# Row maxima of two softmaxes, taken straight from PSUM and turned into a row by one product with ones

## The chip, the cores and the metric

The kernel runs on one core of a Trainium2 chip. The metric is the device time of one execution in microseconds (us), lower is better. TensorE multiplies matrices, VectorE (DVE) and ScalarE (ACT) work on tiles in SBUF and PSUM, GpSimd (POOL) on tiles in SBUF, and DMA queues move data between SBUF and device memory.

## The reference

One layer over 2048 latent tokens and 256 context tokens, width 1024. All tokens are normalised, modulated and projected. Two attentions run on the result: latent attention (MLA, 8 heads, 96 score dimensions, keys are 2048 latent and 256 context tokens) and 2-D neighbourhood attention on a 32 x 64 grid (8 heads, a window of 8 x 16 keys with a learned bias, and all context keys). Both are gated, projected, merged and projected again, then a residual and a norm follow.

```python
def one(qblk):                       # latent attention, one block of queries
    sc = jnp.einsum('bqhd,bkhd->bhqk', qblk, k) * scale
    p = jax.nn.softmax(sc, axis=-1)
    return jnp.einsum('bhqk,bkhd->bqhd', p, v)

# neighbourhood attention, one grid row
s_win = jnp.einsum('bwhd,brwchd->bhwrc', qr, k_win) * scale + bias
s_ctx = jnp.einsum('bwhd,blhd->bhwl', qr, kc) * scale
p = jax.nn.softmax(jnp.concatenate([s_win, s_ctx], axis=-1), axis=-1)
```

## The kernel before, in words

Until about 1062 us the kernel normalises, modulates and projects. From there to about 2255 us stands the attention stretch: both attentions in one stream. After it come the gated output products.

A number is kept as a high and a low part of type fp32r, and a score is the sum of three products (high by high, high by low, low by high).

**Latent attention** (loop at L1242). 32 blocks u, each one head and 512 queries (g). A block has nine key steps kp of 2 x 128 keys. In a step each half makes a transposed score tile S (keys on partitions, 512 queries wide) in PSUM by three products, ScalarE takes the exponential into a tile P (L1274), GpSimd adds P to the running denominator za (L1280, L1282), and every second step TensorE multiplies the collected P by the values (pv, L1225, into oacc). The softmax needs the maximum of each query. It enters the score as a 97th contraction row: the keys have a row of ones, and row 96 of the query tile qh holds minus the maximum. A block's scores can only start when this row is there.

The maxima of block u+1 are made during block u (max_tasks, L809, a list of 13 tasks). For each 128 queries (qt), the scores of high by high are made once more with queries on partitions (pm tiles, 512 keys wide, the last 256). `pair` (L820) makes two of them: ScalarE copies the first to SBUF (L823), VectorE takes a running maximum over the second and the copy (a scan, L825). `rest` (L828) reduces the last 256 keys (L830) and joins both (L831). `fin` (L834) first runs the deferred work (zdefer: the denominators' sums zp of an earlier block), then turns the four columns of maxima into a row by four fp32 products with the identity, L840, each shown as two instructions in the trace, and ScalarE copies the row into qh (L841).

**Neighbourhood attention** (natten, L1026). Per head, 16 query tiles have window products nm and context products nc, whose maxima VectorE takes (n_max, L878). `fin` (L906) joins them once (L908, L909), then turns the 16 columns into rows, four columns at a time (four products nf, L912), and VectorE copies each into QLt (L914). The maxima of head h+1 are made while head h is scored; the four `fin` items come at the start of a head. The work is a generator that yields weights; `feed` (L1167) takes from it twice per key step so that it is spread evenly over the stretch.

**Order.** In the stretch TensorE's matmuls (mm, L804) are pinned in program order. The other engines' instructions are ordered by the scheduler of the framework from priorities and dependences, and each engine then runs its own in order. `more` (L1260) issues the maxima's tasks through the steps of a block; `fin` falls into the last step, behind its first score. PSUM tiles of scores, maxima and neighbourhood scores take turns in five buffers (psm, L140). The maxima of block 0 are issued with a high priority (L1159) and run among the projections, around 863 to 880 us. SBUF space of the attention pools is partly that of the projections' operands.

Of the kernel before, what the change touches and what calls it, by code (L numbers as in the profile page):

```python
# [11 lines left out]
F32 = mybir.dt.float32  # L12
F32R = mybir.dt.float32r
AF = mybir.ActivationFunctionType
ALU = mybir.AluOpType
AX = mybir.AxisListType
# [3 lines left out]
P = 128  # L20
# [6 lines left out]
H = 8  # L27
# [5 lines left out]
DK = NOPE + ROPE  # L33
NB = 4
W = S // NB
NK = S + C
# [28 lines left out]
def tile_hybrid_layer(ctx: ExitStack, tc: tile.TileContext, I: dict, out: bass.AP, dbg=None):  # L65
    nc = tc.nc
# [8 lines left out]
    ident = const.tile([P, P], F32, name="ident")  # L75
# [64 lines left out]
    def psm(name):  # L140
        if env["rot"] is not None:
            env["rot"] = (env["rot"] + 1) % 5
            if env["rot"] >= 3:
                return env["psS"].tile([P, W], F32, tag="S", name=name)
        return psM.tile([P, W], F32, tag="M", name=name)
# [652 lines left out]
        nc.gpsimd.memset(bc(Kh[i][DK:DK + 1, :]), 1.0)  # L798

    zdefer = []  # L800

    pe = {"pin": False}

    def mm(*args, **kw):  # L804
        ins = nc.tensor.matmul(*args, **kw)  # L805
        if pe["pin"]:
            tc.keep_in_program_order(ins)

    def max_tasks(u, qh):  # L809
        i = (u // NB) % 2  # L810
        m1 = mq.tile([P, 4], F32, tag="m1", name=f"m1{u}")
        last = [None] * 4

        def product(qt, ci):
            a, b = ci * W, min(NK, (ci + 1) * W)
            pm = psm(f"pm{u}_{qt}_{ci}")
            mm(pm[:, :b - a], qh[0:DK, qt * P:(qt + 1) * P], Kh[i][0:DK, a:b], start=True, stop=True)
            return pm

        def pair(qt, ci):  # L820
            p0 = product(qt, ci)
            sb = mq.tile([P, W], F32, tag="msb", name=f"msb{u}_{qt}_{ci}")
            nc.scalar.activation(sb, p0, AF.Copy)  # L823
            p1 = product(qt, ci + 1)
            nc.vector.tensor_tensor_scan(sb, p1, sb, -3.0e38 if ci == 0 else last[qt], op0=ALU.max, op1=ALU.max)  # L825
            last[qt] = sb[:, W - 1:W]

        def rest(qt):  # L828
            p0 = product(qt, 4)
            nc.vector.tensor_reduce(m1[:, qt:qt + 1], p0[:, :NK - 4 * W], axis=AX.X, op=ALU.max, negate=True)  # L830
            nc.vector.scalar_tensor_tensor(out=m1[:, qt:qt + 1], in0=last[qt], scalar=-1.0, in1=m1[:, qt:qt + 1],  # L831
                                           op0=ALU.mult, op1=ALU.min)

        def fin():  # L834
            for f in zdefer:
                f()
            zdefer.clear()
            pm = psm(f"pmf{u}")
            for t in range(4):
                mm(pm[DK:DK + 1, t * P:(t + 1) * P], m1[:, t:t + 1], ident, start=True, stop=True)  # L840
            nc.scalar.activation(qh[DK:DK + 1, :], pm[DK:DK + 1, :], AF.Copy)  # L841

        o = []
        for qt in range(4):
            o += [lambda q=qt: pair(q, 0), lambda q=qt: pair(q, 2), lambda q=qt: rest(q)]
        return o + [fin]


    def grid(ap):
# [28 lines left out]
    def n_max(h, bn):  # L878
        mx = nv.tile([P, 2, 16], F32, tag="nmx", name=f"nmx{h}")
        m1 = nv.tile([P, 16], F32, tag="nm1", name=f"nm1{h}")  # L880
        kg = grid(NKm[:, 0:S])
        neg = -3.0e38

        def win(qb):
            rb, cb = divmod(qb, 4)
            (r0, r1), (c0, c1) = NROW[rb], CREG[cb]
            nr, ncl = r1 - r0, c1 - c0
            pm = psm(f"nm{h}_{qb}")
            pv_ = pm[:, :nr * ncl].rearrange("p (r c) -> p r c", c=ncl)
            mm(pv_, NQs[:, qb * P:(qb + 1) * P], kg[:, r0:r1, c0:c1], start=True, stop=True)  # L890
            rr, cc_ = r0 - rb * 8 + 4, c0 - cb * 16 + 8
            jk = npl.tile([P, W], F32, tag="njk", name=f"njk{h}_{qb}", bufs=1)
            nc.vector.tensor_tensor_reduce(
                out=jk[:, :nr * ncl].rearrange("p (r c) -> p r c", c=ncl), in0=pv_,
                in1=bn[:, rr:rr + nr, cc_:cc_ + ncl], scale=1.0, scalar=neg,
                op0=ALU.add, op1=ALU.max, accum_out=mx[:, 0, qb:qb + 1])

        def cmax(b2):
            pm = psm(f"nc{h}_{b2}")
            for x in range(2):  # L900
                qb = 2 * b2 + x
                mm(pm[:, x * C:(x + 1) * C], NQs[:, qb * P:(qb + 1) * P], NKm[:, S:NK],
                                 start=True, stop=True)
            nc.vector.reduce_max(mx[:, 1, 2 * b2:2 * b2 + 2], pm.rearrange("p (x c) -> p x c", x=2), axis=AX.X)

        def fin(rb):  # L906
            if rb == 0:
                nc.vector.tensor_tensor(m1, mx[:, 0, :], mx[:, 1, :], op=ALU.max)  # L908
                nc.vector.tensor_scalar_mul(m1, m1, -1.0)  # L909
            pm = psm(f"nf{h}_{rb}")  # L910
            for cb in range(4):
                mm(pm[64:65, cb * P:(cb + 1) * P], m1[:, rb * 4 + cb:rb * 4 + cb + 1], ident,  # L912
                                 start=True, stop=True)
            nc.vector.tensor_copy(rowcol(QLt[64:65, rb * W:(rb + 1) * W]), blk(pm[64:65, :]))  # L914

        o = []
        for b2 in range(8):
            o += [lambda q=2 * b2: win(q), lambda q=2 * b2 + 1: win(q), lambda b=b2: cmax(b)]
        return o + [lambda r=r: fin(r) for r in range(4)]

    def n_score(d, t):
        h = d["h"]
# [96 lines left out]
            npairs.append([("w", a, cb), ("w", b, cb)])  # L1019

    WT, WM, WI, WP = 1.0, 0.6, 6.0, 16
    n_weight = 24 * WM + H * (24 * WT + 24 * WM + 4 * WM + WI)

    held = []

# [131 lines left out]
    load_rope(1)  # L1157
    env["q"] = nc.sync
    with tc.high_priority(offset=HOIST):  # L1159
        for f in max_tasks(0, qhs[0]):  # L1160
            f()

    env["psS"], env["rot"] = psS, -1
# [78 lines left out]
    for u in range(nu):  # L1242
# [1 line left out]
        i = h % 2  # L1244
        qh, ql = qhs[u], qls[u]
        vt = Vt
        tasks = []
        if u + 2 < nu:
            qhs.append(load_qh(u + 2))
        if u + 1 < nu:  # L1250
            tasks = max_tasks(u + 1, qhs[u + 1])
        if g == NB - 1 and h + 1 < H:
            Vt = load_v(h + 1)
        acc = psO.tile([P, W], F32, tag="O", name=f"oacc{u}")
# [3 lines left out]
        for kp in range(NKP):  # L1258
            pt = mp.tile([P, 2, W], F32, tag="P", name=f"P{u}_{kp}", bufs=PB)
            def more(frac):  # L1260
                nonlocal done
                want = min(len(tasks), int(len(tasks) * (kp + frac) / (NKP - 0.7) + 1))
                while done < want:
                    tasks[done]()
                    done += 1

            for x in range(2):
                ks = slice((2 * kp + x) * P, (2 * kp + x + 1) * P)
                sp = psm(f"S{u}_{kp}_{x}")
                n = 0  # L1270
                for a, b, e in ((Kh[i], qh, DK + 1), (Kh[i], ql, DK), (Kl[i], qh, DK)):
                    mm(sp, a[0:e, ks], b[0:e, :], start=(n == 0), stop=(n == 2))
                    n += 1
                nc.scalar.activation(pt[:, x, :], sp, AF.Exp)  # L1274
                more(0.33 * x)
                if x == 0:
                    feed(total_weight * (step + 0.5 - LEAD) / (nsteps - TAIL - LEAD))
            ve = nc.vector if kp in ZDVE.get(nu - u, ()) else nc.gpsimd
# [259 lines left out]
```

## Time and profile before

| | |
|---|---|
| runs shown, us | 2628.12, 2628.84, 2633.1 (median 2628.84) |
| profiled execution, us | 2630.43, span of the profile 2628.6 |
| mean granted clock of TensorE | 0.994 |
| TensorE busy, share of the span | 2554.9 us, 97% |
| VectorE, ScalarE, GpSimd busy | 1246.7, 1038.4, 1029.1 us |
| instructions | 36044 |

The profiled execution is 1.6 us above the median of the runs. Matmuls overlap each other in the pipeline, so a matmul of 0.40 us duration can be followed by the next after less; the distance of the starts tells what one costs in a stream. A wait is put down to what ended last before the waiting instruction started.

### The profile page before, as it was taken

The numbers are of one execution on the slowest core, as the hardware profiler recorded it, in microseconds if no ns is written. First come the engines' busy times: TensorE is split into PE (matmuls) and PEld (weight loads), VectorE is DVE, ScalarE is ACT, GpSimd is POOL, SyncE is SP. The second block draws the span as 40 slices with busy tenths as digits, with TensorE's granted clock in tenths as the row PEclk, the third lists the DMA queues.
The fourth block names the chain that finished last, engine by engine and source line by source line (L and its number), as shares of the span: only waits on it lengthen the run. The fifth ranks groups of instructions, "written<-read, shape, count | busy, mean of one in ns | idle before, by whom it ended". The sixth has DMA issues, their size and how long they took to land.

```text
span 2628.6 us, 36044 instructions
## 1 busy us (share of the span) xinstructions
PE 2554.9 (97%) x13244; PEld 1857.0 (71%) x13244; DVE 1246.7 (47%) x2132; ACT 1038.4 (40%) x2030; POOL 1029.1 (39%) x797
## 2 busy tenths in 40 slices
PE   7999999999999999899999999999999999999998
PEld 4878888877799788556565656565555565798998
DVE  4653212222300211556665757575756557465654
ACT  4663422212211222355555555455545555222221
POOL 1312111112300000467676767676767676232220
PEclk9999999999999999999999999999999999999999
DMA  7535865456543465704133232414131314765552
GB/s 259 186 90 173 263 218 179 131 181 189 175 132 112 144 209 173 194 16 107 31 81 79 54 84 48 112 32 107 38 90 44 80 48 161 226 194 182 165 161 69
DMA packets 182985, 342.94 MB, mean 130 GB/s; under 512 B 25130, under 2 KB 95950, under 8 KB 175438
## 3 DMA queue, kind: packets, MB, share of 16 engines
q1 hardware_dynamic: 168872, 299.01, 38.3%
q0 software_dynamic: 13504, 41.35, 5.5%
q8 instruction: 104, 1.70, 0.3%
q14 instruction: 73, 0.60, 0.1%
q10 hardware_dynamic: 432, 0.28, 0.0%
HBM read 214.42 MB, written 126.13 MB: 130 GB/s over the span
## 4 chain that ended last, share of the span: by engine, by line
PE 85%; DVE 8%; DMA 2%; issue 2%; ACT 1%; SPq 0%; POOL 0%; DVEq 0%; ACTq 0%; POOLq 0%
PE accm L135 25%; PE S L805 13%; PE oacc L805 10%; PE pm L805 6%; PE ya L135 5%; PE f L135 5%; PE vacc L135 4%; PE nacc L226 3%; DVE msb L825 3%; PE no L805 3%; PE accf L135 2%; DVE m L831 2%; PE accx L135 1%; PE nf L805 1%; PE qa_False L135 1%
## 5 line engine op out<-in xcount | busy, mean ns | idle before, releaser
L1282 POOL TENSOR_TENSOR za<-za,P 128x1024 f32<-128x1024 f32 x217 | 515.4, 2375 | 203.2 <-ACT P L1274 200.2
L1274 ACT ACTIVATE P<-S 128x512 f32<-128x512 f32 x576 | 340.8, 595 | 237.6 <-PE S L805 227.9
L135 PE MATMUL accm<-hh,whi 128*128 128x512 f32 x928 | 366.7, 395 | 0.0
L135 PE MATMUL accm<-hl,whi 128*128 128x512 f32 x928 | 366.6, 395 | 0.0
L135 PE MATMUL accm<-hh,wlo 128*128 128x512 f32 x928 | 366.4, 395 | 0.0
L805 PE MATMUL oacc<-P,V 128*64 128x512 f32 x1152 | 285.8, 612 | 0.0
L805 PE MATMUL S<-qh,Kh 97*128 97x512 f32 x576 | 239.3, 415 | 13.6 <-ACT msb L823 4.0
L825 DVE TENSOR_TENSOR_SCAN msb<-pm,msb 128x512 f32<-128x512 f32 x128 | 155.8, 1217 | 161.1 <-ACT msb L823 139.4
L805 PE MATMUL S<-ql,Kh 96*128 96x512 f32 x576 | 229.4, 398 | 0.0
L805 PE MATMUL S<-qh,Kl 96*128 96x512 f32 x576 | 228.0, 396 | 0.0
L823 ACT ACTIVATE msb<-pm 128x512 f32<-128x512 f32 x256 | 151.9, 594 | 177.0 <-PE pm L805 170.4
L805 PE MATMUL pm<-Kh,qh 96*128 96x512 f32 (+1 forms) x640 | 215.1, 401 | 6.3 <-DVE msb L825 4.6
L825 DVE TENSOR_TENSOR_SCAN msb<-pm,msb,msb 128x512 f32<-128x512 f32 x128 | 163.8, 1280 | 88.9 <-ACT msb L823 87.5
L135 PEld LDWEIGHTS accm<-hh,whi 128*128 128x128 f32 x928 | 174.1, 188 | 42.8 <-issue 0.8
L135 PEld LDWEIGHTS accm<-hh,wlo 128*128 128x128 f32 x928 | 174.1, 188 | 42.2
L135 PEld LDWEIGHTS accm<-hl,whi 128*128 128x128 f32 x928 | 174.1, 188 | 42.0 <-issue 0.4
L805 PEld LDWEIGHTS pm<-Kh,qh 96*128 96x128 f32 x640 | 111.1, 189 | 114.1 <-issue 45.8
L135 PE MATMUL ya<-u,woh 128*128 128x256 f32 x1024 | 185.0, 283 | 0.5 <-DVE frt L126 0.4
L135 PE MATMUL f<-wfh,y 128*128 128x512 f32 (+1 forms) x528 | 161.2, 384 | 2.9 <-DMA wfh<-wfS 2.0
L805 PEld LDWEIGHTS oacc<-P,V 128*64 128x64 f32 x1152 | 69.2, 137 | 133.5 <-issue 132.5
L135 PEld LDWEIGHTS ya<-u,woh 128*128 128x128 f32 x1024 | 160.1, 192 | 1.6 <-DVE t L1340 0.9
L831 DVE SCALAR_TENSOR_TENSOR m<-msb,m 128x1 f32<-128x1 f32 x128 | 157.6, 1231 | 2.1
(1929 smaller groups left out, 4622.5 us busy)
## 6 DMA issues: line engine op xcount, KB each, us to landing
rawc<-in_wch SPq DMA_DIRECT2D x30, 512.0 KB
KA<-kB SPq DMA_DIRECT2D x16, 576.0 KB
xl<-in_xb SPq DMA_DIRECT2D x32, 256.0 KB
wm<-in_wmodb SPq DMA_DIRECT2D x8, 1024.0 KB
kmS<-sk POOLq DMA_DIRECT2D x32, 256.0 KB, 3.8
qR<-q SPq DMA_DIRECT2D x16, 512.0 KB
qm<-sq POOLq DMA_DIRECT2D x32, 256.0 KB, 4.0
woS<-ps SPq DMA_DIRECT2D x16, 512.0 KB
```

The costliest lines, as they stand in the source:

```text
L135: nc.tensor.matmul(acc, a, b, start=(i == 0), stop=(i == n - 1))
L226: nc.tensor.matmul(acc[:, :n], a[:, k, sl], b[:, k, :n], start=(k == 0 and q == 0), stop=(k == KT - 1 and q == 2))
L805: ins = nc.tensor.matmul(*args, **kw)
L823: nc.scalar.activation(sb, p0, AF.Copy)
L825: nc.vector.tensor_tensor_scan(sb, p1, sb, -3.0e38 if ci == 0 else last[qt], op0=ALU.max, op1=ALU.max)
L831: nc.vector.scalar_tensor_tensor(out=m1[:, qt:qt + 1], in0=last[qt], scalar=-1.0, in1=m1[:, qt:qt + 1], op0=ALU.mult, op1=ALU.min)
L1274: nc.scalar.activation(pt[:, x, :], sp, AF.Exp)
L1282: ve.tensor_tensor(za, za, pt, op=ALU.add)
```

## The change

In the latent attention each pm tile is reduced by VectorE straight from PSUM into one of 20 columns (4 query groups by 5 key pieces); there are 20 such tasks. A 21st, `fold`, reduces five to one with a minus sign and lets GpSimd spread the result: identity times column, a 128 x 4 x 128 tile whose column sums are the turned row. `row` multiplies it by a matrix of ones in one fp32r product of 512 columns and copies row 96 of the result into qh; then the deferred work runs. `row` is issued in the last key step behind its first score. The tasks are paced so that they end earlier (NKP - 2.0 for NKP - 0.7). In the neighbourhood attention the joint maximum becomes one reduction, four spreads go to GpSimd (two buffers), and each `fin` becomes one product with ones; the items are five, with spread k and product k - 1 in item k.

```diff
     zdefer = []
+    onesr = mz.tile([P, P], F32R, name="onesr", bufs=1)
+    nc.vector.tensor_copy(onesr, ones)
...
+    def spread(dst, col):
+        nc.gpsimd.tensor_tensor(dst, ident.unsqueeze(1).to_broadcast([P, 4, P]), col.unsqueeze(2).to_broadcast([P, 4, P]),
+                                op=ALU.mult)
+
     def max_tasks(u, qh):
         i = (u // NB) % 2
+        m5 = mq.tile([P, 4, 5], F32, tag="m5", name=f"m5{u}")
         m1 = mq.tile([P, 4], F32, tag="m1", name=f"m1{u}")
-        last = [None] * 4
-
-        def product(qt, ci):
+        md = mq.tile([P, 4, P], F32R, tag="md", name=f"md{u}", bufs=1)
+
+        def part(qt, ci):
             a, b = ci * W, min(NK, (ci + 1) * W)
             pm = psm(f"pm{u}_{qt}_{ci}")
             mm(pm[:, :b - a], qh[0:DK, qt * P:(qt + 1) * P], Kh[i][0:DK, a:b], start=True, stop=True)
-            return pm
-
-        def pair(qt, ci):
-            p0 = product(qt, ci)
-            sb = mq.tile([P, W], F32, tag="msb", name=f"msb{u}_{qt}_{ci}")
-            nc.scalar.activation(sb, p0, AF.Copy)
-            p1 = product(qt, ci + 1)
-            nc.vector.tensor_tensor_scan(sb, p1, sb, -3.0e38 if ci == 0 else last[qt], op0=ALU.max, op1=ALU.max)
-            last[qt] = sb[:, W - 1:W]
-
-        def rest(qt):
-            p0 = product(qt, 4)
-            nc.vector.tensor_reduce(m1[:, qt:qt + 1], p0[:, :NK - 4 * W], axis=AX.X, op=ALU.max, negate=True)
-            nc.vector.scalar_tensor_tensor(out=m1[:, qt:qt + 1], in0=last[qt], scalar=-1.0, in1=m1[:, qt:qt + 1],
-                                           op0=ALU.mult, op1=ALU.min)
-
-        def fin():
+            nc.vector.reduce_max(m5[:, qt, ci:ci + 1], pm[:, :b - a], axis=AX.X)
+
+        def fold():
+            nc.vector.tensor_reduce(m1, m5, axis=AX.X, op=ALU.max, negate=True)
+            spread(md, m1)
+
+        def row():
+            pm = psm(f"pmf{u}")
+            mm(pm, onesr, md.rearrange("p t f -> p (t f)"), start=True, stop=True)
+            nc.scalar.activation(qh[DK:DK + 1, :], pm[DK:DK + 1, :], AF.Copy)
             for f in zdefer:
                 f()
             zdefer.clear()
-            pm = psm(f"pmf{u}")
-            for t in range(4):
-                mm(pm[DK:DK + 1, t * P:(t + 1) * P], m1[:, t:t + 1], ident, start=True, stop=True)
-            nc.scalar.activation(qh[DK:DK + 1, :], pm[DK:DK + 1, :], AF.Copy)
...
+        return [lambda q=qt, c=ci: part(q, c) for qt in range(4) for ci in range(5)] + [fold], row
...
+        mds = [None] * 4
+
+        def turn(rb):
+            if rb == 0:
+                nc.vector.tensor_reduce(m1, mx.rearrange("p t q -> p q t"), axis=AX.X, op=ALU.max, negate=True)
+            mds[rb] = npl.tile([P, 4, P], F32R, tag="nmd", name=f"nmd{h}_{rb}")
+            spread(mds[rb], m1[:, rb * 4:rb * 4 + 4])
+
         def fin(rb):
-            if rb == 0:
-                nc.vector.tensor_tensor(m1, mx[:, 0, :], mx[:, 1, :], op=ALU.max)
-                nc.vector.tensor_scalar_mul(m1, m1, -1.0)
             pm = psm(f"nf{h}_{rb}")
-            for cb in range(4):
-                mm(pm[64:65, cb * P:(cb + 1) * P], m1[:, rb * 4 + cb:rb * 4 + cb + 1], ident,
-                                 start=True, stop=True)
+            mm(pm, onesr, mds[rb].rearrange("p t f -> p (t f)"), start=True, stop=True)
             nc.vector.tensor_copy(rowcol(QLt[64:65, rb * W:(rb + 1) * W]), blk(pm[64:65, :]))
...
-        return o + [lambda r=r: fin(r) for r in range(4)]
+
+        def last(k):
+            if k < 4:
+                turn(k)
+            if k > 0:
+                fin(k - 1)
+
+        return o + [lambda k=k: last(k) for k in range(5)]
...
-    n_weight = 24 * WM + H * (24 * WT + 24 * WM + 4 * WM + WI)
+    n_weight = 24 * WM + H * (24 * WT + 24 * WM + 5 * WM + WI)
...
-                want = min(len(tasks), int(len(tasks) * (kp + frac) / (NKP - 0.7) + 1))
+                want = min(len(tasks), int(len(tasks) * (kp + frac) / (NKP - 2.0) + 1))
...
+                if x == 0 and kp == NKP - 1 and row is not None:
+                    row()
```

## Rows read from the trace of the kernel before

**Rows 1.** The page: busy time of each engine, and the chain by engine.

```profile
PE 2554.9 (97%) x13244; PEld 1857.0 (71%) x13244; DVE 1246.7 (47%) x2132; ACT 1038.4 (40%) x2030; POOL 1029.1 (39%) x797
...
PE 85%; DVE 8%; DMA 2%; issue 2%; ACT 1%; SPq 0%; POOL 0%; DVEq 0%; ACTq 0%; POOLq 0%
```

**Rows 2.** Busy time by stretch: length, busy by engine, clock, DMA share, GB/s.

```profile
core 0: us, PE busy (x) PEld busy (x) DVE busy (x) ACT busy (x) POOL busy (x), PEclk, DMA share, GB/s
...
1062.00:2255.00 1193.00, 1148.15 (x5758) 688.15 (x5756) 745.71 (x1061) 623.22 (x1138) 802.95 (x453) 0.99 0.31 78
```

**Rows 3.** Timeline of TensorE at the latent attention's turned rows, three blocks.

```profile
1135.59 0.82 PE L805 MATMUL pmf<-ident,m 128*1 128x128 f32 x6
1137.46 0.38 PE L805 MATMUL pmf<-ident,m 128*1 128x128 f32 x2 [1.05 <-DVE m L831]
...
1511.57 1.04 PE L805 MATMUL pmf<-ident,m 128*1 128x128 f32 x8
1512.54 0.50 PE L805 MATMUL S<-qh,Kh 97*128 97x512 f32 x1
...
2225.16 0.82 PE L805 MATMUL pmf<-ident,m 128*1 128x128 f32 x6
```

**Rows 4.** Timeline of TensorE at a turned row of the neighbourhood attention.

```profile
1385.30 0.39 PE L805 MATMUL S<-ql,Kh 96*128 96x512 f32 x1
1385.54 0.39 PE L805 MATMUL S<-qh,Kl 96*128 96x512 f32 x1
1385.85 1.03 PE L805 MATMUL nf<-ident,nm 128*1 128x128 f32 x8
1386.82 0.50 PE L805 MATMUL S<-qh,Kh 97*128 97x512 f32 x1
1387.16 0.40 PE L805 MATMUL S<-ql,Kh 96*128 96x512 f32 x1
```

**Rows 5.** Waits of TensorE, 1062 to 2255 us: us in total, times, longest.

```profile
PE pmf L805 <- DVE m L831: 15.9, 19, 1.4
PE S L805 <- ACT msb L823: 4.0, 2, 2.8
PE pm L805 <- DVE msb L825: 3.2, 11, 0.6
PE S L805 <- DVE msb L825: 3.1, 8, 0.6
PE nf L805 <- DVE nm L909: 2.6, 1, 2.6
```

**Rows 6.** Groups by line over the span: busy us, mean ns, idle before.

```profile
L825 DVE TENSOR_TENSOR_SCAN msb<-pm,msb,msb 128x512 f32<-128x512 f32 x128 | 163.8, 1280 | 88.9 <-ACT msb L823 87.5 <-PE ns_('w', 2, 2)_13301 L805 0.3
...
L831 DVE SCALAR_TENSOR_TENSOR m<-msb,m 128x1 f32<-128x1 f32 x128 | 157.6, 1231 | 2.1
...
L825 DVE TENSOR_TENSOR_SCAN msb<-pm,msb 128x512 f32<-128x512 f32 x128 | 155.8, 1217 | 161.1 <-ACT msb L823 139.4 <-PE S L805 14.7 <-PE pm L805 6.2
...
L904 DVE TENSOR_REDUCE nmx<-nc 128x2 f32<-128x512 f32 x64 | 43.6, 681 | 37.5 <-PE nc L805 37.5
...
L1180 POOL TENSOR_TENSOR za<-za 128x512 f32<-128x512 f32 x31 | 39.9, 1287 | 2.4
...
L1238 DVE TENSOR_TENSOR or<-oacc,or 64x512 f32<-64x512 f32 x32 | 21.8, 683 | 16.5 <-ACT or L1237 16.1
```

**Rows 7.** Timeline of GpSimd beside the turned rows of rows 3.

```profile
1130.46 2.37 POOL L1282 TENSOR_TENSOR za<-za,P 128x1024 f32<-128x1024 f32 x1 [0.19 <-ACT P L1274]
1135.04 2.34 POOL L1282 TENSOR_TENSOR za<-za,P 128x1024 f32<-128x1024 f32 x1 [2.21 <-ACT P L1274]
...
1508.51 2.39 POOL L1282 TENSOR_TENSOR za<-za,P 128x1024 f32<-128x1024 f32 x1
...
2224.89 2.34 POOL L1282 TENSOR_TENSOR za<-za,P 128x1024 f32<-128x1024 f32 x1 [2.43 <-ACT P L1274]
```

**Rows 8.** Timeline of VectorE: the joining of maxima in the first and second block.

```profile
868.06 0.16 DVE L831 SCALAR_TENSOR_TENSOR m<-msb,m 128x1 f32<-128x1 f32 x1
...
1135.36 2.04 DVE L831 SCALAR_TENSOR_TENSOR m<-msb,m 128x1 f32<-128x1 f32 x1
```

**Rows 9.** Timeline of GpSimd: the first load of the values.

```profile
1062.43 0.56 POOL L792 DMA_DIRECT2D V<-vaS  x1 [209.20 <-PE S L805]
```

**Rows 10.** Timeline of VectorE: the neighbourhood's joint maximum of one head.

```profile
1353.60 0.16 DVE L908 TENSOR_TENSOR nm<-nmx 128x16 f32<-128x16 f32 x1
```

More of the change, by code (lines that the diff above doesn't have):

```diff
@@ L837, in fin @@
             zdefer.clear()
-            pm = psm(f"pmf{u}")
-            for t in range(4):
-                mm(pm[DK:DK + 1, t * P:(t + 1) * P], m1[:, t:t + 1], ident, start=True, stop=True)
-            nc.scalar.activation(qh[DK:DK + 1, :], pm[DK:DK + 1, :], AF.Copy)
[L843 to L846, printed above, removed]
+        return [lambda q=qt, c=ci: part(q, c) for qt in range(4) for ci in range(5)] + [fold], row
     def grid(ap):
@@ L1159, in tile_hybrid_layer @@
     with tc.high_priority(offset=HOIST):
-        for f in max_tasks(0, qhs[0]):
+        tasks, row = max_tasks(0, qhs[0])
+        for f in tasks + [row]:
             f()
@@ L1246, in tile_hybrid_layer @@
         vt = Vt
-        tasks = []
+        tasks, row = [], None
         if u + 2 < nu:
@@ L1250, in tile_hybrid_layer @@
         if u + 1 < nu:
-            tasks = max_tasks(u + 1, qhs[u + 1])
+            tasks, row = max_tasks(u + 1, qhs[u + 1])
         if g == NB - 1 and h + 1 < H:
```

## The prediction

> **What bounds the kernel now.** I read the page's busy line first, then the chain, then the stretch that the change touches. TensorE is busy 2554.9 of 2628.6 us and the chain that ended last is 85% TensorE [rows 1]. So a microsecond taken off TensorE's stream counts, and work on the other engines counts only where TensorE waits for it. In the attention stretch TensorE is busy 1148.15 of 1193.00 us at a granted clock of 0.99, which leaves 45 us idle; VectorE, ScalarE and GpSimd are busy 63%, 52% and 67% of it [rows 2]. The rest of the kernel holds no code that changes, except the first query block's maxima. Since TensorE's matmuls are pinned in program order there, any operand that comes late stops everything behind it. A difference of 0.2%, 5 us, is about what a measurement of this kernel can tell from no change.
>
> **The two turned rows.** Today four fp32 products, eight instructions in the trace, turn four columns of maxima into a row. In the latent attention the group begins at 1511.57 and the next score begins at 1512.54: 0.97 us [rows 3]. The neighbourhood's group takes the same, 1385.85 to 1386.82 [rows 4]. The replacement is one fp32r product of 128x512, the form of the scores, which follow each other at 0.24 us (1385.30 to 1385.54) [rows 4]. There are 32 groups of each kind (32 query blocks; 8 heads by 4), so 64 x (0.97 - 0.24) = 46.7 us leave the stream. The new weights have 128 columns instead of one; their load lies under the product before, as the scores' loads do.
>
> Changing between fp32 and fp32r costs something too: the group starts 0.31 us after the last score instead of 0.24, and the first score after it takes 0.34 us to the next [rows 4]. That is 0.17 to 0.18 us, which goes only where no other fp32 work stands beside the group. In the latent attention the denominators' sums (zp) stand there before and after. Of the 32 neighbourhood groups I count 20: eight stand beside nz, some adjoin each other. 20 x 0.18 = 3.6 us; the bounds are 0 and 32 x 0.18 = 5.8.
>
> **The waits that go.** The list of TensorE's waits in the stretch has 15.9 us for the turned row's maxima, 4.0 and 3.2 and 3.1 for the ScalarE copies and scans that empty the maxima's PSUM tiles, and 2.6 for the neighbourhood's maxima: 28.8 us [rows 5]. All of these operations are removed. The first is worth a look. The small operation on L831 handles one column, takes 0.16 us in the first block, and 1231 ns on average later [rows 6, 8]. In the second block it starts at 1135.36, lasts 2.04 us and ends at 1137.40, with GpSimd's sum, which runs from 1135.04 to 1137.38 [rows 7, 8]; TensorE waited 1.05 us for it [rows 3]. It reads two tiles from SBUF, and so does GpSimd. The new fold on VectorE is a reduction with one input. If it is held like L831, it takes some 1.1 us more; spread over 31 blocks that is up to 34 us on the path. I take 0.16 us, because the row nearest in operands, a reduction, shows no such stretching: L904 has 681 ns for 512 columns [rows 6], though from PSUM.
>
> The Trainium skill, "SBUF — State Buffer", section "Who interferes with whom", says that a VectorE instruction with two SBUF inputs contends with GpSimd instructions that read SBUF, the second to come waits for the whole of the other, and tensor_reduce never contends on trn2. The rows on L831 agree; that the fold escapes no row shows. By that rule the sum below stands; without it the time would be 2603.
>
> **VectorE and ScalarE.** Per 128 queries, the change removes two copies on ScalarE, scans of 1217 and 1280 ns and L831, and adds four reductions of 512 columns instead, for which L904's 681 ns is the price [rows 6]: 2.72 against 3.73 us, over 128 groups about 130 us less on VectorE, and more than that on ScalarE. This lies beside TensorE, so I cost it at nothing; its cover is TensorE's own stream, and it would cost only if a PSUM tile were emptied later than now. It is emptied sooner: today a pair needs a copy and then a scan, from now on each product has its own 0.68 us. I leave 3 us for waits of this kind, between 0 and the 10.3 us that they have now (4.0 + 3.2 + 3.1).
>
> **GpSimd: the new wait.** Each spread is a 128x512 product with two inputs, for which L1180 gives 1287 ns [rows 6]. 64 of them are 82 us, which takes GpSimd from 803 to 885 us of 1193; it doesn't become the bound, but it is a queue in order, and TensorE now waits for its end. The row's product stands where it stood, in the last key step behind the first score; the spread comes out one step earlier. Ahead of it on GpSimd is the denominator's sum of the step before, behind it the next one; between them GpSimd idles 2.21 us [rows 7], enough for 1.29. In the second block the earlier sum ends at 1132.83, so the spread could end near 1134.2, and the row is wanted at 1135.59 [rows 3, 7]. In a crowded block the sum ends at 1510.90 and the row is wanted at 1511.57 [rows 3, 7]: 0.6 us late. The bounds are 0 and the 3.1 to 3.4 us of the slower rival below; nearer the first, I take 0.25 us x 31 = 8 us. For the neighbourhood the maxima are ready long before: its fold L908 ran at 1353.60, the group it feeds at 1385.85 [rows 4, 10]. So two of four spreads (two buffers) can run ahead, the other two have one to two half steps for 1.29 us and perhaps a sum of 2.37 in front. Bounds 0 and 1.3 us; I take 0.2 x 32 = 6 us.
>
> The Trainium skill, "GPSIMD Engine Reference", section "Engine selection", sends elementwise work to VectorE, as two-input operations take about twice as long on GpSimd. The trace agrees, 1287 against 683 ns [rows 6]. If every spread's extra 0.6 us reached TensorE, 64 of them would cost 38 us instead of my 14, and the time would be 2593.
>
> **The first block.** The new matrix of ones is a tile of a pool that opens behind the value tiles. Their load was issued only at 1062.43, after 209.20 us of waiting [rows 9]; I read this as their space being in use until the projections end. So the ones can come only then, and the first row with them, in front of the first score. I estimate 2 us for the copy of the ones, a product (0.40 us in [rows 4]), the row's copy on ScalarE and the handovers. Bounds 0 (the space is free earlier) and 5. The other changes, a weight of 5 instead of 4 items in the feeding and maxima that finish a step earlier, move work within the stretch; cost 0, as TensorE has the same work to fill it.
>
> **The sum.** -46.7 - 3.6 - 28.8 + 3 + 8 + 6 + 2 = -60.1 us. The profiled execution took 2630.43 us, so 2570.3; the median of the runs is 1.6 us below the profiled execution, so 2569.
>
> **Rivals.** *The waits change their names* (0.2): all 28.8 us come back at the spreads and the reductions in place of my 17. Then -46.7 - 3.6 + 2 = -48.3, 2580. For it: 45 idle microseconds in a stretch with every engine over half busy. Against: the largest named one has a cause that is removed.
>
> *Fold or spread late in most blocks* (0.12): the 34 us above, 2603.
>
> *Slower: the spread stands behind the next sum on GpSimd* (0.08). The engines other than TensorE aren't pinned, so the order is the scheduler's. In the second block that sum ends at 1137.38 and the row is wanted at 1135.59; with 1.29 for the spread TensorE waits 3.1 us. In the last such block the sum ends at 2227.23, the row is wanted at 2225.16: 3.4 us [rows 3, 7]. 31 blocks by 3.2 are 99 us in place of the 8: 2569 + 91 = 2660. It decides from a mean wait at the row of (60.1 + 8) / 31 = 2.2 us on. Against it: the spread comes first in program order and the sum waits for an exponential.
>
> *It doesn't do what it says* (0.05): the stretch is held by something besides TensorE, and shorter products only lengthen idle time; 2629. The 96% busy share speaks against.
>
> **The numbers.** The forecast has 0.55. Range: without new waits and with all idle time gone it would be 2630.4 - 46.7 - 3.6 - 45, near 2535, which is unlikely to the last microsecond; I set 2540. At the top it takes in 2603 and reaches 2606. Outside lie the slower rival, the no-change case and some of the tail. Faster by over 0.2%: 0.55 + 0.2 + 0.12 = 0.87; slower 0.08, same 0.05.
>
> **What would show it.** Right: 32 products each for pmf and nf, the next score 0.24 us behind; no L823, L825 or L831; TensorE's busy time about 50 us lower; idle time in the stretch near 30 us; waits at pmf and nf for GpSimd's spreads together about 14 us; the new reductions near 0.68 us and the fold near 0.2. Wrong: a spread that starts right behind the last or next-to-last sum of a block with TensorE idle at pmf for over 1 us each time; a fold of over 1 us; a gap of over 5 us at the first score.

## The result, and the profile after

The changed kernel takes 2570.08 us, the median of four runs (2569.03 to 2572.13), beside 2629.74 us for the kernel before (2628.12 to 2633.1, four runs): ratio 0.9772, 95% interval [0.9756, 0.9789], faster. The profiled execution took 2569.03 us with a span of 2567.2 us at a mean granted clock of 0.987; before it was 2628.6 us at 0.994.

The page, busy time and chain of the kernel after (before: [rows 1]):

```profile
PE 2505.7 (98%) x12796; PEld 1839.1 (72%) x12796; DVE 1102.7 (43%) x2285; ACT 905.3 (35%) x1774; POOL 1092.2 (43%) x861
...
PE 88%; DVE 3%; DMA 3%; POOL 2%; issue 2%; ACT 1%; SPq 1%; POOLq 0%; ACTq 0%; DVEq 0%
```

TensorE has 448 instructions fewer (64 rows, seven fewer each) and its rows in the trace are busy 49.2 us less. VectorE loses 144 us, ScalarE 133, GpSimd gains 63; VectorE's part of the chain falls from 8% to 3%. So the time still follows TensorE, as forecast. Its busy time by stretch:

```profile
core 0: us, PE busy (x) PEld busy (x) DVE busy (x) ACT busy (x) POOL busy (x), PEclk, DMA share, GB/s
...
1062.00:2195.00 1133.00, 1104.04 (x5361) 672.32 (x5361) 603.92 (x1208) 492.09 (x887) 861.22 (x514) 0.98 0.32 81
```

The attention stretch shrank by about 60 us, about the whole gain, and its idle time from 45 to 29 us [rows 2]. Cut at TensorE's own products instead of at round numbers, the span falls by 61.4 us like this: 62.9 from the first score to the last (1189.0 to 1126.1), and 5.1 among the projections, where the first block's maxima stand (from one and the same projection product, at 856.54 us before and 856.01 after, to the last, at 1061.74 and 1056.07). Lost are 1.5 at the first score and 5.6 behind the last one; the start, up to the first projection product, is 0.6 shorter. The stretch's clock is 0.98 instead of 0.99, which no term of the sum held. What TensorE waits for there (us in total, times, longest; before: [rows 5]):

```profile
PE pmf L807 <- POOL md L812: 11.8, 6, 3.0
PE S L807 <- DVE m L825: 4.3, 7, 1.0
PE pm L807 <- DVE m L825: 3.3, 3, 1.8
PE nf L807 <- POOL nmd L812: 2.8, 1, 2.8
```

The waits for the joining, the copies and the scans are gone. The rows now wait for GpSimd's spreads, rarely but long: 6 waits of 2 us on average, where L831 had 19 of 0.8. The operations that replaced the old ones, grouped by line (as [rows 6], here from 1055 to 2200 us alone):

```profile
L825 DVE TENSOR_REDUCE m<-pm 128x1 f32<-128x512 f32 x496 | 330.2, 686 | 306.0 <-PE pm L807 301.4
...
L812 POOL TENSOR_TENSOR nmd<-ident,nm 128x512 fp32r<-128x512 f32 x32 | 33.0, 1041 | 4.9 <-PE nf L807 4.7
L812 POOL TENSOR_TENSOR md<-ident,m 128x512 fp32r<-128x512 f32 x31 | 32.3, 1042 | 7.7 <-DVE m L828 7.5
```

And TensorE at the first score and at one late row (timeline):

```profile
1056.07 0.39 PE L135 MATMUL accm<-hh,wlo 128*128 128x512 f32 x1
1056.64 0.47 PE L807 MATMUL pmf<-md,onesr 128*128 128x512 f32 x1 [0.18 <-DVE onesr L802]
1057.81 0.50 PE L807 MATMUL S<-qh,Kh 97*128 97x512 f32 x1 [0.70 <-ACT qh L834]
...
1338.49 0.51 PE L807 MATMUL pmf<-md,onesr 128*128 128x512 f32 x1 [2.09 <-POOL md L812]
```

The first score begins 1.74 us after the last projection product (0.23 before), close to the forecast's 2 us for the late ones. The late row at 1338.49 is explained by GpSimd's timeline: both spreads that a neighbourhood's head can run ahead, and one of its sums, stood in front of the latent one.

```profile
1334.22 1.04 POOL L812 TENSOR_TENSOR nmd<-ident,nm 128x512 fp32r<-128x512 f32 x1
1335.22 1.22 POOL L956 TENSOR_TENSOR nza<-nza,np_('w', 1, 1)_10796 128x480 f32<-128x480 f32 x1
1336.40 1.04 POOL L812 TENSOR_TENSOR nmd<-ident,nm 128x512 fp32r<-128x512 f32 x1
1337.40 1.04 POOL L812 TENSOR_TENSOR md<-ident,m 128x512 fp32r<-128x512 f32 x1
```

The fold (L828) was ready at 1334.69; the first of these neighbourhood spreads is for a product at 1365.64, 30 us later. What that wait costs is more than its 2.09 us, as the stretches around it show:

```profile
core 0: us, PE busy (x) PEld busy (x) DVE busy (x) ACT busy (x) POOL busy (x), PEclk, DMA share, GB/s
...
1065.00:1070.00 5.00, 5.00 (x12) 2.54 (x13) 1.29 (x2) 1.19 (x2) 2.95 (x2) 0.50 1.04 225
...
1336.40:1338.40 2.00, 0.00 (x1) 0.00 (x0) 0.08 (x1) 1.09 (x2) 2.00 (x4) 1.00 0.01 4
1341.00:1343.50 2.50, 2.50 (x8) 0.66 (x6) 0.00 (x0) 0.88 (x2) 2.50 (x3) 0.50 0.53 150
1344.00:1347.00 3.00, 3.00 (x25) 2.26 (x21) 1.17 (x2) 0.94 (x2) 3.00 (x3) 1.00 0.96 231
```

At 1336.4 TensorE stands still for 2 us, goes on at the full clock, and 2 us later is granted the lower level, 1.2 GHz, while it is busy without a gap. The first line is the same behind three waits of the first block. There are eight such places in this stretch, 44.4 us in sum, against four and 20.5 us before. Three of the eight follow a wait at pmf and one the wait at nf; the longest, 13.7 us from 1511.2, follows waits of 0.75 us for ScalarE and 0.40 us for a reduction. So the spreads are not the only cause. An estimate of the clock's price over a whole run is (1 - mean granted clock) x span: 33.4 us after, 15.8 before (the clock is given to 0.001, so each is good to some 1.3 us). Of the 17.6 us between them about 12 lie in the stretch (half of 44.4 less half of 20.5); the rest lies in the run's first 50 us and behind the last score.

### The profile page after: what moved, and what is told of

Its sections match the earlier page's. It is cut to its first block, busy times and chain, and to the rows that moved or that the text cites. A ratio compares the mean times of both kernels' runs of the same rounds, so it can differ in the third digit from the quotient of the medians.

```text
span 2567.2 us, 34839 instructions
## 1 busy us (share of the span) xinstructions
PE 2505.7 (98%) x12796; PEld 1839.1 (72%) x12796; DVE 1102.7 (43%) x2285; ACT 905.3 (35%) x1774; POOL 1092.2 (43%) x861
## 4 chain that ended last, share of the span: by engine, by line
PE 88%; DVE 3%; DMA 3%; POOL 2%; issue 2%; ACT 1%; SPq 1%; POOLq 0%; ACTq 0%; DVEq 0%
PE accm L135 25%; PE S L807 15%; PE oacc L807 10%; PE pm L807 6%; PE f L135 5%; PE ya L135 4%; PE vacc L135 4%; PE nacc L226 3%; PE no L807 3%; PE accf L135 2%; PE accx L135 1%; PE qa_False L135 1%; PE pstl L185 1%; PE nm L807 1%; POOL za L1288 1%
## 5 line engine op out<-in xcount | busy, mean ns | idle before, releaser
L825 DVE TENSOR_REDUCE m<-pm 128x1 f32<-128x512 f32 (+1 forms) x640 | 387.6, 632 | 420.0 <-PE pm L807 414.3
L807 PE MATMUL oacc<-P,V 128*64 128x512 f32 x1152 | 292.0, 624 | 0.0
L807 PE MATMUL pm<-Kh,qh 96*128 96x512 f32 (+1 forms) x640 | 222.6, 395 | 4.5 <-DVE m L825 3.3
L807 PEld LDWEIGHTS pm<-Kh,qh 96*128 96x128 f32 x640 | 121.1, 189 | 106.7 <-issue 62.5
L807 PEld LDWEIGHTS S<-qh,Kh 97*128 97x128 f32 x576 | 109.9, 191 | 54.0 <-issue 12.4
L135 PE MATMUL ya<-u,wol 128*128 128x256 f32 x512 | 144.8, 283 | 0.0
L356 ACT ACTIVATE g<-accm 128x512 f32<-128x512 f32 x88 | 52.2, 593 | 248.8 <-PE accm L135 202.6
```

Of the source, the lines that this page charges most:

```text
L135: nc.tensor.matmul(acc, a, b, start=(i == 0), stop=(i == n - 1))
L356: nc.scalar.activation(s1, acc, AF.Sigmoid)
L825: nc.vector.reduce_max(m5[:, qt, ci:ci + 1], pm[:, :b - a], axis=AX.X)
```

## The experiments

The theory: the gain is TensorE's own instructions plus the waits on VectorE and ScalarE, less what the spreads make it wait. The rivals: the reductions alone carry it, the new pace carries it, or the waits only change their names. Every kernel is compared with the kernel before on its own chip, and stands as a diff against the kernel after unless said otherwise. In the working, "idle" is span less TensorE's busy time and "clock" the estimate above. Each working rests on one trace per kernel, and up to the first projection product, which no edit reaches, these traces take between 57.5 and 64.4 us. From there to the first block's maxima all take 792.1 to 792.3 us.

**1. Reductions without the new rows.** Both rows are made as before, by four fp32 products, and the spreads are left out (the neighbourhood's `fin` and its weight are those of before). The new pace (NKP - 2.0) and the deferred work behind the row stay in.

```diff
-            spread(md, m1)
...
-            mm(pm, onesr, md.rearrange("p t f -> p (t f)"), start=True, stop=True)
+            for t in range(4):
+                mm(pm[DK:DK + 1, t * P:(t + 1) * P], m1[:, t:t + 1], ident, start=True, stop=True)
```

> The changed kernel with its reductions from PSUM kept, but both turned rows made as before by four fp32 products with the identity (no spread, no ones). My theory (sum of terms): 46.7 + 3.6 us of TensorE's instructions come back, the 14.6 us that TensorE waits for GpSimd's spreads in the changed kernel go, so 2570 + 36 = 2606 us, TensorE busy about 50 us more than 2505.7, no wait at pmf or nf over 3 us in sum. Rival (the gain is the faster emptying of PSUM and the absence of scans, the products with ones bring little): within 6 us of 2570.

Measured: 2590.83 us, ratio 0.9851 [0.9822, 0.988], between the two. Its page:

```profile
PE 2543.6 (98%) x13244; PEld 1865.3 (72%) x13244; DVE 1117.1 (43%) x2292; ACT 905.9 (35%) x1774; POOL 1030.6 (40%) x797
```

Between the kernels it splits the gain in two steps (us, from span, busy time and clock of the three profiled executions):

| | before | reductions, old rows | after |
|---|---|---|---|
| span | 2628.6 | 2591.2 | 2567.2 |
| idle | 73.7 | 47.6 | 61.5 |
| clock | 15.8 | 23.3 | 33.4 |
| busy less clock | 2539.1 | 2520.3 | 2472.3 |

The first step takes 26 us of idle time, and also 19 us of busy time less clock (11.3 of busy time as it stands) although no TensorE instruction went (13244 in both). That is waiting which the matmul rows don't show. The weight-load rows do; before, in the attention stretch, and then here:

```profile
PEld pmf L805 <- DVE m L831: 21.4, 19, 1.6
PEld pm L805 <- DVE msb L825: 21.4, 34, 1.6
...
PEld S L805 <- DVE msb L825: 10.0, 19, 1.0
```

```profile
PEld S L805 <- DVE m L822: 9.9, 17, 1.6
...
PEld pm L805 <- DVE m L822: 5.5, 4, 2.0
```

For pm behind the scans the loads have 21.4 us where the matmul rows have 3.2 [rows 5]: a load can stand still while the product before it is still shown as busy. The products' starts bear this out. Of two pm products of 512 columns in a row with no idle time shown between them, 127 of 250 pairs start more than 0.28 us apart before, and 3 of 120 here. Summed over all products in front of a pm, at the full clock, the distance beyond the usual one of the same two forms is an estimated 18 us before and under 2 here, most of the 19.

Not all of this step is the reductions' own, since the pace went in with them. The kernel before with an earlier pace alone (NKP - 1.2, experiment 2) loses all its waits for L831 and 11 us of idle time as well (62.7). It keeps the hidden time, though (17 us by the same sum), and its busy time less clock is 2540.0. So the 19 us are the reductions', while the 26 us are theirs and the pace's together; no run has the reductions and the old rows at the old pace. The new rows then take 48 us of busy time and give back 14 in idle time and 10 in clock: 24 net.

**2. The new rows alone.** Copies, scans and the joining stay as before (the functions of the kernel before, with the fold reduced to its spread); both rows are new.

```diff
-            nc.vector.reduce_max(m5[:, qt, ci:ci + 1], pm[:, :b - a], axis=AX.X)
+            return pm
...
-            nc.vector.tensor_reduce(m1, m5, axis=AX.X, op=ALU.max, negate=True)
```

> The changed kernel with its products with ones kept, but the latent maxima taken as before by ScalarE copies, scans and the small joining operation. My theory: the three PSUM waits of before (4.0, 3.2, 3.1 us) replace the 8.4 us of the reductions, and the joining operation is held by GpSimd's sums, so that the spread comes later by about 1 us in most blocks: 2575 to 2600 us, with more than 11.8 us of wait at pmf. Rival (emptying PSUM is what paid): above 2610.

Measured: 2640.65 us, 1.0039 [1.0022, 1.0056]: a miss, on the rival's side (above 2610). TensorE is busy 2538.9 us, 16 less than before, yet it waits for the scans:

```profile
PE pm L807 <- DVE msb L832: 21.7, 23, 2.0
PE S L807 <- DVE msb L832: 16.8, 33, 1.7
```

I took the pace (NKP - 2.0), which crowds the scans, for the cause, and put it between the two:

```diff
-                want = min(len(tasks), int(len(tasks) * (kp + frac) / (NKP - 2.0) + 1))
+                want = min(len(tasks), int(len(tasks) * (kp + frac) / (NKP - 1.2) + 1))
```

> The kernel with copies and scans kept and products with ones, its 13 tasks now paced by NKP - 1.2 instead of NKP - 2.0, so that the pairs of products are crowded less and the spread is still issued a step ahead of the row. My theory: what made that kernel 2641 us is the crowding; the waits of TensorE's products for scans fall from about 45 us (21.7 + 16.8 and smaller ones) to below 25, and the time to 2595 to 2620 us. Rival (scans and rows with ones don't go together at any pace, as the spread waits behind the joining operation): 2630 us or more, with more wait at pmf than the 4.0 us it had.

Measured: 2622.04 us, 0.9968 [0.9955, 0.9981], 2 us above what was expected, and the waits for scans are still over 30 us: a near miss. Its counterpart is the kernel before with this pace alone (the same line, NKP - 0.7 to NKP - 1.2):

> The kernel before with nothing changed but the pace of its 13 tasks (NKP - 1.2 instead of NKP - 0.7), the pace of the run at 2622 us that had scans and products with ones. My theory: it is the crowding of copies and scans that ate the gain of the products with ones there (some 21 us where the reductions stand), so this kernel alone is slower than before by about the difference: 2635 to 2650 us, with over 25 us of waits of TensorE for scans and copies, against 12 before. Rival (the pace is harmless, it is the products with ones that don't pay beside scans): within 5 us of before, 2625 to 2635.

Measured: 2616.89 us, 0.9947 [0.9929, 0.9966]. Theory and rival both missed, and crowding alone falls as an explanation: an earlier pace helps the kernel before. Its joining, grouped by line:

```profile
L831 DVE SCALAR_TENSOR_TENSOR m<-msb,m 128x1 f32<-128x1 f32 x128 | 69.5, 543 | 2.4
```

L831 takes 543 ns on average instead of 1231 [rows 6], and no wait at pmf for it is left. So part of the 15.9 us [rows 5] could have been had by one number.

Against that, the new rows beside scans gain nothing (0.9968 to 0.9947, and the intervals overlap). With them busy time less clock is lower by 52.6 us (2487.4 against 2540.0), about what the rows take elsewhere; idle time is higher by 30 us and the clock's share by 34. One cause is a confound of my own. In both kernels with scans and new rows the first block's maxima no longer run among the projections but behind them (timeline of TensorE, the kernel with NKP - 1.2):

```profile
1065.31 0.58 PE L807 MATMUL pm<-Kh,qh 96*128 96x256 f32 x1 [0.26 <-ACT msb L830]
1068.69 0.79 PE L807 MATMUL pmf<-md,onesr 128*128 128x512 f32 x1 [2.81 <-POOL md L812]
1070.17 0.79 PE L807 MATMUL S<-qh,Kh 97*128 97x512 f32 x1 [0.68 <-ACT qh L847]
```

and most of that is at 1.2 GHz (stretch from 1055 to 1074 us):

```profile
1055.00:1074.00 19.00, 13.09 (x26) 7.63 (x27) 11.60 (x16) 6.56 (x11) 1.03 (x1) 0.50 1.03 233
```

That the copies' tiles and md together no longer fit beside the projections' operands is argued, not shown. The first score then stands 20.9 us behind the last projection product instead of 0.2, while the projections are shorter by 9.4 us: a net loss of 11 us, about the whole difference of the two spans (2624.8 and 2613.2). From the first score to the last the two take the same time (1175.5 and 1176.1). How the rest of the 64 us divides between the scans and the spreads stays open.

**3. The neighbourhood's rows as before**, the latent ones new.

```diff
-            mm(pm, onesr, mds[rb].rearrange("p t f -> p (t f)"), start=True, stop=True)
+            for cb in range(4):
+                mm(pm[64:65, cb * P:(cb + 1) * P], m1[:, rb * 4 + cb:rb * 4 + cb + 1], ident,
+                                 start=True, stop=True)
```

> The changed kernel with the neighbourhood attention's turned rows as before (16 columns joined by two operations, four fp32 products per row), the latent attention as changed. My theory: half of the instructions come back, 32 x 0.73 + 3.6 = 27 us, less 2.8 us of wait for spreads: 2570 + 24 = 2594 us. Rival (the neighbourhood's spreads, which GpSimd runs early, delay the sums and the latent spreads and cost what they save): 2570 to 2580.

Measured: 2581.76 us, 0.9817 [0.9791, 0.9842]. The neighbourhood's new rows are worth 12 us, half of what was expected and nearer to the rival. They take 32.5 us of busy time less clock (2504.8 to 2472.3); idle time gives back 6.7 and the clock 12.8. The latent rows wait only 3.8 us for their spreads here, against 11.8: without the neighbourhood's spreads GpSimd's queue is free for theirs.

**4. The spreads on VectorE.**

```diff
-        nc.gpsimd.tensor_tensor(dst, ident.unsqueeze(1).to_broadcast([P, 4, P]), col.unsqueeze(2).to_broadcast([P, 4, P]),
+        nc.vector.tensor_tensor(dst, ident.unsqueeze(1).to_broadcast([P, 4, P]), col.unsqueeze(2).to_broadcast([P, 4, P]),
```

> The changed kernel with all 64 spreads on VectorE instead of GpSimd. My theory: a spread is 0.69 us of VectorE plus the time in which GpSimd's sums hold it back (both read two SBUF tiles), about 1.1 us on average as for the small joining operation of before; the wait of 11.8 us at pmf changes by less than 8 us in either direction, 2562 to 2578 us, and single spreads last up to 3 us. Rival by the rule that elementwise work belongs on VectorE, which is twice as fast: the 14.6 us of waits for GpSimd go and some low-clock time with them, 2550 us.

Measured: 2564.35 us, 0.975 [0.9722, 0.9778], as the theory has it; the interval overlaps that of the kernel after. Groups by line:

```profile
L812 DVE TENSOR_TENSOR nmd<-ident,nm 128x512 fp32r<-128x512 f32 x32 | 47.2, 1492 | 0.6
L812 DVE TENSOR_TENSOR md<-ident,m 128x512 fp32r<-128x512 f32 x32 | 30.0, 938 | 1.0
...
L828 DVE TENSOR_REDUCE m<-m 128x4 f32<-128x20 f32 x32 | 5.4, 169 | 0.4
```

The shortest spread takes 0.68 us on VectorE, the longest 2.87; the fold, right before it and with one input, takes 169 ns on average and 174 at most. The Trainium skill, "SBUF — State Buffer", section "Who interferes with whom", has this difference: a VectorE instruction with two SBUF inputs contends with GpSimd's reads, tensor_reduce does not. The trace agrees on both. By "GPSIMD Engine Reference", section "Engine selection", the Trainium skill would put such a product on VectorE; alone it is faster there, but held by GpSimd it takes 1492 and 938 ns on average against 1041 there, and the runs show no clear gain. TensorE's waits for spreads move, from 11.8 and 2.8 us (pmf, nf) to 3.3 and 8.9.

**5. The row half a step later**, behind the second score of the last step.

```diff
-                if x == 0 and kp == NKP - 1 and row is not None:
+                if x == 1 and kp == NKP - 1 and row is not None:
```

> The changed kernel with the row's product half a key step later (behind the second score of a block's last step). My theory: the 11.8 us of wait at pmf fall below 2 us, and the stretches at 1.2 GHz that follow four of these waits go (about 8 us), so 2570 - 20 = 2550 us. Rival (the row is then late for the next block's first score, which waits for ScalarE's copy): new waits of S for the copy into qh, 2565 to 2575 us.

Measured: 2549.32 us, 0.970 [0.968, 0.9721]: the time as expected, the wait not. It still has 7.4 us at pmf (5 times). Of the 21 us of span gained in the trace, 6.1 lie in the start, up to the first projection product (63.79 us after, 57.71 here), and are not the edit's. From the first score to the last it gains 17.1: 4.6 of idle time, an estimated 5 of clock (34.1 us at 1.2 GHz instead of 44.4), and the rest of busy time, which no run explains.

**6. The ones early**, in a pool whose space is free during the projections.

```diff
-    onesr = mz.tile([P, P], F32R, name="onesr", bufs=1)
+    onesr = mq.tile([P, P], F32R, name="onesr", bufs=1)
```

> The changed kernel with the matrix of ones in a pool whose space is free while the projections run. My theory: the first block's row is made among the projections, the gap before the first score (1.7 us from the last projection's start to the first score's start in the changed kernel, 0.24 before) goes, 2568 us, hardly measurable; in the trace the first pmf stands near 880 us. Rival (the space was not what held it): pmf stays near 1057 us.

Measured: 2563.0 us (2557.31 to 2568.42), 0.9752 [0.9723, 0.978]; it overlaps the kernel after. The first row now runs at 870.99 among the projections, and the first score follows the last projection product by 0.24 us. So late ones are the cause of the gap of 1.74 us. Of the 11.7 us by which this trace is shorter than that of the kernel after, 6.3 lie in the start, and the four runs themselves fall into two pairs 10 us apart; that the ones bring more than the gap is not shown.

**7. Every spread done twice** (the same product written again).

```diff
+        for _ in range(2):
```

> The changed kernel with each of the 64 spreads done twice on GpSimd, one after the other into the same tile. My theory: GpSimd gets 67 us more work and stays below TensorE, but a latent spread ends 1.04 us later, against 0.05 to 1.3 us in hand before the row is wanted in the changed kernel: 0.6 us more in most of 31 blocks, up to 3 us in the neighbourhood's first row, and some time at 1.2 GHz: 2590 to 2605 us, wait at pmf 30 us or more. Rival (GpSimd's queue has room, the spreads are hidden): within 6 us of 2570.

Measured: 2635.62 us, 1.0038 [1.0025, 1.0051], 31 us above the expected range: a miss in size. The waits are where the theory has them, and dearer. Against the kernel after idle time rises by 46 us and the clock's share by 19 (0.980). All waits of TensorE for the spreads:

```profile
PE pmf L807 <- POOL md L813: 48.3, 27, 5.9
PE nf L807 <- POOL nmd L813: 13.3, 9, 4.8
```

**8. The old pace**, NKP - 0.7, with everything else new: the fold then falls into the last step, right ahead of its row.

```diff
-                want = min(len(tasks), int(len(tasks) * (kp + frac) / (NKP - 2.0) + 1))
+                want = min(len(tasks), int(len(tasks) * (kp + frac) / (NKP - 0.7) + 1))
```

> The changed kernel with the old pace of the maxima's tasks (NKP - 0.7), so that the fold and the spread are issued in the last key step directly ahead of the row. My theory: TensorE then waits in each block for a reduction (0.4), a fold (0.2), a spread (1.0) and often for a sum on GpSimd that stands in front: about 2 us each, 31 x 2 = 62 in place of 11.8, and time at 1.2 GHz behind it: 2620 to 2660 us. Rival (only the products and the reductions count, the pace nothing): 2565 to 2580 us.

Measured: 2718.71 us, 1.0338 [1.0311, 1.0366]; right in direction, too small in size. Waits of TensorE, then GpSimd at one row:

```profile
PE pmf L807 <- POOL md L812: 109.1, 31, 6.0
```

```profile
1485.45 2.35 POOL L1288 TENSOR_TENSOR za<-za,P 128x1024 f32<-128x1024 f32 x1 [0.28 <-ACT P L1278]
1487.77 1.03 POOL L812 TENSOR_TENSOR md<-ident,m 128x512 fp32r<-128x512 f32 x1
```

The fold began at 1486.22; the sum had GpSimd until 1487.80, and the row waited until 1488.86. After this wait too the clock falls, here to 1.2 GHz with TensorE busy throughout:

```profile
1486.20:1488.80 2.60, 0.00 (x0) 0.00 (x0) 0.18 (x2) 0.91 (x2) 2.60 (x3) 1.00 0.00 0
1489.00:1495.00 6.00, 6.00 (x22) 2.59 (x24) 0.69 (x1) 1.47 (x3) 2.50 (x2) 0.50 0.24 67
```

The waits at pmf are 97 us above the kernel after, and the clock (0.959 on the page) costs 78 us more by the estimate, which overlaps other terms somewhat: the span grew by 153.

**9. Together.** Row late and ones early (the diffs of 5 and 6):

> The changed kernel with the row half a key step later and the matrix of ones in space that is free early. My theory: both gains add, 2549 - 3 = 2546 us, within 2540 to 2550. Rival (the second gain was noise): 2549 us or more.

Measured: 2545.09 us (2541.38 to 2551.25), 0.9678 [0.9661, 0.9696], as expected, and the lowest median of the study, ahead of both kernels. Its interval overlaps that of experiment 5, so that the second gain adds to the first is not shown. The same with the latent spreads on VectorE and the neighbourhood's on GpSimd:

```diff
-            spread(md, m1)
+            spread(md, m1, nc.vector)
...
-            spread(mds[rb], m1[:, rb * 4:rb * 4 + 4])
+            spread(mds[rb], m1[:, rb * 4:rb * 4 + 4], nc.gpsimd)
```

> As the last kernel, with the latent attention's spreads on VectorE and the neighbourhood's left on GpSimd. My theory: the waits at pmf that the late row left (7.4 us in 5 blocks, where GpSimd had the neighbourhood's spreads in front) fall below 2 us, the wait at nf stays near 2.8, and some time at 1.2 GHz goes: 2537 to 2545 us. Rival (VectorE's spreads, held by GpSimd's sums, delay its reductions and so the PSUM tiles): waits for the reductions above 12 us, 2546 us or more.

Measured: 2548.24 us, 0.9691 [0.9677, 0.9704], above the expected range and, within what the runs can tell, the same as the first of the two. The wait at pmf fell from 6.5 to 2.0 us, but one score now waits 4.3 us for VectorE's L953: a wait that changed its name. VectorE's timeline has the cause, a spread of 6.28 us right in front of L953:

```profile
1960.92 6.28 DVE L812 TENSOR_TENSOR md<-ident,m 128x512 fp32r<-128x512 f32 x1
1967.13 0.65 DVE L953 TENSOR_TENSOR np_('w', 1, 2)_16416<-ns_('w', 1, 2)_16415,bt 128x480 f32<-128x480 f32 x1
```

When it began GpSimd was in a sum (1958.82 to 1961.19), and then ran two neighbourhood spreads and two more sums without a pause until 1966.65. The spread, which takes 0.68 us at the shortest (experiment 4), ended 0.55 us behind them. This is the rival's mechanism, VectorE held by GpSimd, in one place.

## Why the prediction was right, and where two errors met

2569 us against 2570.08: the sign, the place and the mechanism hold, but the match to a microsecond is partly luck. By its steps:

- **The rows' instructions**, -46.7 and -3.6 for the changes of type: -50.3. The step from the reductions with old rows to the kernel after takes 48.0 us of busy time less clock. Right in sum. By experiment 3 it divides as 15.5 for the latent rows and 32.5 for the neighbourhood's, where I had about half each; why, no run settled.
- **The waits that go**, -28.8, with +3 for new ones: -25.8. Measured by the first step: 26.1 us of idle time and 18.8 of busy time, -44.9. This term was too small: I read the waits in the matmul rows alone, and those of the weight loads held more. It also has the wrong owner in part: by the kernel with the pace alone, the waits for L831 go with the pace, which I had costed at 0. And 4.0 us of the step lie among the projections, where the first block's maxima run and where I had expected no gain. The new waits behind reductions were 8.4 us (4.3, 3.3 and 0.8 for nc), not 3.
- **The fold**, 0.16 us: 169 ns. The rival at 2603 is out.
- **The spreads**, +8 and +6: 11.8 and 2.8 in the matmul rows (16.8 and 4.0 in those of the loads). The sum holds, the details less: a spread takes 1041 ns, not L1180's 1287, and only 6 of 31 blocks wait, when other spreads or sums stand in front. My reasoning for the neighbourhood, that two spreads can run ahead, was right and overlooked its other side: on GpSimd's queue those two pass in front of a latent one that is wanted at once (1338.49).
- **The first block**, +2: the gap is 1.74 us. Not foreseen were the block's waits for reductions right behind it (1061.65 to 1064.53, 2.1 us) and the lower clock behind them (0.50 from 1065 to 1070).
- **Missing: the clock.** The stretch's busy time was priced as if the clock could not change. By the estimate it costs 17.6 us more after than before over the run, about 12 of them in the stretch. From the first score to the last 20.5 us ran at 1.2 GHz before, 34.1 with the reductions and the old rows (experiment 1) and 44.4 after, so more than half of the rise came with no spread in the kernel.

Together: -44.9 - 48.0 + 13.9 (idle time of the second step, 8.0 of it between the first score and the last and 0.9 at the first) + 17.6 = -61.4, the difference of the spans. This adds up by the way the parts are defined and proves none of them. A term too small by 19 and a missing one of up to 18 cancelled.

Of the rivals, names of waits did change in part (14.6 us at the spreads and 8.4 at the reductions, 23 in place of 28.8), but the hidden 19 us did not come back. The slower one, spread behind the next sum, was not this kernel's case; experiment 8 shows that it is real. It was to decide from a mean wait of 2.2 us at the row; with 31 waits of 3.5 us on average that kernel is slower than before. What keeps the change on the fast side is the pace, NKP - 2.0. I had costed it at 0 as a mere move of work, though the 8 us for the spreads rested on it (the spread one step earlier).

## What to carry to other kernels

Read the waits of the weight loads beside those of the matmuls before pricing what goes: a load that stands still can hide in a busy TensorE. When a helper engine gets a new job on the path, give it lead time in the program (the fold a step early, the row half a step late) before looking for a faster engine, and look at what else that queue may run ahead of it. Before crediting a whole gain to an edit, see in the trace where the time went: here up to 7 us between two traces lay in front of any changed instruction. Price a TensorE wait in a dense stream above its own length, because the clock may fall behind it.

## What the runs showed of the hardware that was not expected

- **The clock falls inside a busy stream.** Among kernels with the same TensorE instructions, much more waiting at the two rows went with less clock: 9.3 us and 0.992 (experiment 9, first kernel), 14.6 and 0.987 (after), 61.6 and 0.980 (every spread twice), about 112 and 0.959 (old pace). The sum alone doesn't order small differences: 13.7 us went with 0.991 (experiment 6) and 12.2 with 0.992 (experiment 4), scans beside new rows had 0.983 at 15.3, and the kernel before waited more in shorter pieces and had 0.994.
- **Order alone can be worth as much as work.** Half a step for one product (experiment 5) gave 17 us from the first score to the last, 0.7%, with not an instruction changed, some 5 us of it by the clock.
- **One VectorE instruction can be held through several of GpSimd's.** A spread with two SBUF inputs took 6.28 us while GpSimd went through five instructions (experiment 9, second kernel), against 0.68 at the shortest (experiment 4).
- **A GpSimd product with broadcast inputs is cheaper than a sum of the same size**: 1041 ns against 1282 for L1184 in the same trace. No run here separates the operation from its operands.
